# Seven products for every MLP pair, one buffer for two hidden tiles, and two low weight parts per step by ScalarE and an accumulating DMA

## The chip, the cores and the metric

The kernel runs on one core of a Trainium2 chip. The metric is the device time of one execution in microseconds (us). Three runs of the kernel before took 2107.08, 2108.14 and 2108.43 us; the median is 2108.14.

The engines are PE (TensorE, matmuls), PEld (its weight loads), DVE (VectorE), ACT (ScalarE), POOL (GpSimd, which here only issues DMAs) and SP (which issues the loads of weights). All 16 DMA engines serve the DMAs of SP and POOL.

## The reference

Two decoder layers over 256 tokens and a model width of 2048: a gated short convolution and an MLP, then shared keys and values, stick-breaking attention and a second MLP, each inside norms and a residual. The change lies in the two MLPs:

```
def sq_relu_mlp(u, w_up, w_down):
    return jnp.square(jax.nn.relu(u @ w_up)) @ w_down
```

with u of 256 x 2048, w_up of 2048 x 8192 and w_down of 8192 x 2048, in float32.

## The kernel before

**Two parts.** Each float32 factor is split into a rounded high part and a low part, the rest. A product is three matmuls: high by high, high by low, low by high. For weights, `high_parts` has ACT write the rounded copy (`whi`, L173), and `low_part` has DVE subtract it from the raw weight (`wlo`, L184).

**The stream of weights.** All weights come in chunks of 128 x 1024 (512 KB), in the order of use. SP loads them into five raw buffers (`RAW`, L157), in order. A raw buffer is free once both parts of its chunk are made. The parts lie in a ring of seven high and seven low buffers (`RING`). `chunk(i)` splits up to four chunks ahead of the one that PE uses (`AHEAD`).

**The steps of an MLP.** The 8192 hidden columns are cut into eight blocks of 8 tiles of 128 (`STEPS`). In step e, for e = 0 to 6, PE makes block e + 1 of the hidden layer (up) and multiplies block e by its rows of w_down (down), so the two alternate. A step has two halves h = 0 and 1, for the two halves of the output columns, and a half has four slots: `whole_up` makes one hidden tile from two chunks (16 matmuls of 512 columns at L1013 with high parts, 16 of 256 columns at L1020 with low parts), then `Down.pair` multiplies two hidden tiles by two chunks. A step thus takes 32 chunks, numbered from its base: in each slot two of up, then two of down. The up tile always uses PSUM bank 2 (`UP_BANK`); ACT copies its second half (`half`, L1026), DVE adds that to the first (`s`, L966), and only then may the next up tile start in that bank.

**Eight or seven products.** A pair of hidden tiles by a pair of weight chunks is a 2 x 2 by 2 x 2 block product: the token blocks by the tiles, the tiles by column halves. `Down.eight` does it in eight products. `Down.seven` does it in seven by a scheme with sums of blocks: of the weights, four differences on DVE (L210, in `split_seven`), and of the hidden tiles, four sums (`four_sums`, L271). There are 512 + 3 x 1024 weight columns to split then, in place of 2 x 1024. `SEVEN` says which pairs of which step take seven: in even steps all four, in odd steps pairs 1 to 3, while pair 0 takes eight, in both halves. Pair 0 comes first in half 0 and last in half 1 (`ORDER`). In step 7 pair 0 takes seven in the first half alone, in another order of work.

**Hidden tiles.** `Hidden.tile` makes relu and square on ACT in a buffer `s` of 256 columns (three of them), then splits. Of a seven pair, the even tile has its first 128 columns split by themselves, the odd tile is split whole, and then the four sums are made and split (128 and 384 columns). A pair with eight has a difference per tile (`dif`, L984) split.

**Results.** The products of the scheme that belong to several outputs are copied by ACT once per step (L1088) and added into the running results by nine accumulating DMAs of 256 KB, which POOL issues (`add_behind`, L1033), one at each up tile and each pair that follows: eight of them in half 1, the ninth at the start of half 0.

**Order.** PE runs in the order of the program. The other engines' instructions are ordered by a planner from their priorities and estimated times; each engine then runs its list in order.

Of the kernel before, what the change touches and what calls it, by code (L numbers as in the profile page):

```python
# [46 lines left out]
STEPS = 8  # L47
# [1 line left out]
UP_BANK = 2  # L49
DOWN_BANKS = {(0, 0): 3, (0, 1): 4, (1, 0): 5, (1, 1): UP_BANK, 1: 6, 5: 7, 6: 0, 7: 1}  # L50
LAST_BANKS = [[6, 7], [0, 1]]
SEVEN = [((0, 1, 2, 3),) * 2 if e % 2 == 0 else ((1, 2, 3),) * 2 for e in range(STEPS - 1)] + [((0,), ())]
ORDER = ((0, 1, 2, 3), (1, 2, 3, 0))

IN_N = [j * KD + i for i in range(KD) for j in range(3)]
# [40 lines left out]
def trunk(ctx, tc, x, xT, vecs, rows, ws, out):  # L96
    nc = tc.nc
# [49 lines left out]
    sevens = {}  # L147

    def load_one():
        i = count["loaded"]  # L150
# [10 lines left out]
    def pieces_of(i):  # L161
        w, c = stream[i]
        gains = w.gains(c) if w.gains else [None] * (4 if i < FIRST else 1)
        n = CW // len(gains)
        return [(slice(j * n, (j + 1) * n), gain) for j, gain in enumerate(gains)]

    def high_parts(i):
        while count["loaded"] <= i:
            load_one()
        hi = wsplit.tile([P, CW], F32R, tag="hi", name=f"whi{i}")  # L170
        lo = wsplit.tile([P, CW], F32R, tag="lo", name=f"wlo{i}")
        for j, (at, gain) in enumerate(pieces_of(i)):
            rounded = nc.scalar.activation(  # L173
                hi[:, at], raw[i][:, at], AF.Copy, scale=1.0 if gain is None else gain
            )
# [77 lines left out]
    def split_tile(xs, k, src):  # L253

        hi, lo = xs[k // 4][:, k % 4, 0, :, :], xs[k // 4][:, k % 4, 1, :, :]
        src = src.rearrange("p (b t) -> p b t", b=NB)
        nc.scalar.activation(hi, src, AF.Copy)
        nc.vector.tensor_tensor(lo, src, hi.bitcast(F32), op=ALU.subtract)
# [428 lines left out]
    W = {"in": Weights(ws["in"]), "out": Weights(ws["out"])}  # L687
# [235 lines left out]
    with tc.tile_pool(name="p_in", bufs=1, reuse_waits="tile") as tmp:  # L923
        y = convolution(tmp)
# [14 lines left out]
    def mlp(pool, i, before, after):  # L939
        u = before.x4  # L940
        part = [[None] * 4 for _ in range(NB)]
        held = {}
        scale = [None] * NB

        def two_parts(parts, src):
            hi, lo = parts
            nc.scalar.activation(hi, src, AF.Copy)
            nc.vector.tensor_tensor(lo, src, hi.bitcast(F32), op=ALU.subtract)

        class Hidden:  # L950


            def __init__(self, e):
                self.xs, self.sums = [None] * (NF // 4), {}
                first, second = SEVEN[e]
                self.pairs = [2 * m for m in first]
                self.apart = [2 * m for m in first if m not in second]
                self.eights = [2 * m for m in range(4) if m not in first] if e < STEPS - 1 else []

            def x(self, n, b):  # L960
                return [part_of(self.xs, n, b, j) for j in range(2)]

            def tile(self, n, ps, half):
                s = pool.tile([P, T], F32, tag="s", name="s", bufs=3)
                with tc.high_priority():
                    nc.vector.tensor_tensor(s[:], ps[:, :T], half[:], op=ALU.add)  # L966
                nc.scalar.activation(s[:], s[:], AF.Relu)  # L967
                nc.scalar.activation(s[:], s[:], AF.Square)
                if self.xs[n // 4] is None:
                    self.xs[n // 4] = operand("hid4")  # L970
                if n in self.pairs and n not in self.apart:
                    two_parts(self.x(n, 0), s[:, :P])
                else:
                    split_tile(self.xs, n, s[:])
                if n in self.pairs:
                    held[n] = s
                elif n - 1 in self.pairs:
                    self.sums[n - 1] = self.sums_of(n - 1, held.pop(n - 1), s)
                elif n - n % 2 in self.eights:
                    if n % 2 == 0:  # L980
                        self.sums[n] = pool.tile([P, 2, 2, P], F32R, tag="d", name="sums", bufs=1)
                    parts = [self.sums[n - n % 2][:, n % 2, j, :] for j in range(2)]
                    d = pool.tile([P, P], F32, tag="dif", name="dif", bufs=1)
                    nc.vector.tensor_tensor(d[:], s[:, :P], s[:, P:], op=ALU.subtract)  # L984
                    two_parts(parts, d[:])

            def sums_of(self, n, x, y):
# [3 lines left out]
                if n in self.apart:  # L991
                    one = pool.tile([P, 2, 2, P], F32R, tag="d", name="sums", bufs=1)
                    one = [one[:, 0, j, :] for j in range(2)]
# [112 lines left out]
        class Down:  # L1106


            def __init__(self, j, plan):
                self.j, self.plan, self.ps = j, plan, {}  # L1110
                sevens_at = [at for at in plan if at[1] in SEVEN[at[0]][at[2]]]
                whole_at = [at for at in plan if at not in sevens_at and at[0] == STEPS - 1]
# [6 lines left out]
            def products(self, key, own, at, factors):  # L1119

                begin, end = self.range[own]
                if key not in self.ps:
                    self.ps[key] = bank(DOWN_BANKS[key], "acc" if own == "sum" else "more")
                for n, ((xh, xl), (hi, lo)) in enumerate(factors):
                    first, last = at == begin and n == 0, at == end and n == len(factors) - 1
                    nc.tensor.matmul(self.ps[key][:], xh, hi, start=first, stop=False)  # L1126
                    nc.tensor.matmul(self.ps[key][:], xh, lo, start=False, stop=False)  # L1127
                    self.done = nc.tensor.matmul(self.ps[key][:], xl, hi, start=False, stop=last)  # L1128

            def pair(self, at, first, xs):  # L1130
# [23 lines left out]
            def eight(self, at, first, xs, n):  # L1154
                ws = [chunk(first + t) for t in range(2)]

                def products(key, own, x, c):
                    self.products(key, own, at, [
                        (x(t), [w[:, c * HALF : (c + 1) * HALF] for w in ws[t]]) for t in range(2)
                    ])  # L1160

                products((0, 0), "sum", lambda t: xs.x(n + t, 0), 0)
                products((1, 0), "sum", lambda t: xs.x(n + t, 1), 0)
                if at[0] == STEPS - 1:
                    products((0, 1), "sum", lambda t: xs.x(n + t, 0), 1)
                    products((1, 1), "whole", lambda t: xs.x(n + t, 1), 1)
                else:
                    products((0, 1), "sum", lambda t: [xs.sums[n][:, t, j, :] for j in range(2)], 1)
                    products(5, "fifth", lambda t: xs.x(n + t, 1), 1)
# [314 lines left out]
```

## Time and profile before

| | |
|---|---|
| median of three runs | 2108.14 us |
| profiled execution | 2106.03 us |
| its span, first to last instruction | 2104.3 us |
| its mean granted PE clock | 0.998 |

The profile gives busy times as shares of the span. A row of a view by line names a line of the kernel, an engine, the operation, what it writes and reads, a count, and times. A timeline row has the start and the length in us from the span's start; consecutive instructions overlap by some 0.08 us, so the distance of starts says what an engine pays for one. PE rows of the same line stand merged. In the timelines chunk names are numbers: step 4 of the first MLP has its base at 272. The name `wlo282u` is a low part of the pair of chunks 282 and 283: a for the first half of 282, b for 283, t and u for the differences. `more` and `mg` are the results that the accumulating DMAs read and write, `raw` the loaded weights.

### The profile page before, as it was taken

What the parts mean: (1) busy time and instruction counts of PE and PEld (TensorE: products, weight loads), DVE (VectorE), ACT (ScalarE), POOL (GpSimd) and SP (SyncE); (2) the same over time, 40 slices, a digit from 0 to 9 for tenths busy, and PEclk for the clock granted to TensorE, in tenths of its full rate; (3) what the DMA queues carried; (4) which work ended last, traced back from release to release, by engine and by line L of the source; (5) the groups of instructions that cost most, each with busy time, mean ns of one, the idle gap of its engine ahead of it and who ended that gap; (6) DMA issues with size and microseconds to landing.
All of it is one profiled execution on the core that took longest, in us unless ns stands there. A gap on an engine that the chain in (4) does not pass through costs nothing.

```text
span 2104.3 us, 29885 instructions
## 1 busy us (share of the span) xinstructions
PE 2089.1 (99%) x10608; PEld 1782.1 (85%) x10608; DVE 1837.6 (87%) x2807; ACT 1437.4 (68%) x2210; POOL 112.9 (5%) x137
## 2 busy tenths in 40 slices
PE   9999999999999999999999999999999999999998
PEld 7888888888888888888888888889888888888886
DVE  8999965999899999999766777558999999999997
ACT  8666544776776776767567888547867767677673
POOL 0000000000100101001000000000001010010010
PEclk9999999999999999999999999999999999999999
DMA  8467674577878868779575555655687687786784
GB/s 291 151 205 250 196 258 143 187 234 229 233 220 233 248 204 244 229 228 257 180 224 168 160 160 161 220 179 171 187 254 227 217 248 221 228 253 208 231 241 162
DMA packets 132342, 449.23 MB, mean 213 GB/s; under 512 B 14816, under 2 KB 15072, under 8 KB 131168
## 3 DMA queue, kind: packets, MB, share of 16 engines
q1 hardware_dynamic: 113184, 406.55, 60.1%
q0 software_dynamic: 18720, 40.38, 9.5%
q8 instruction: 83, 1.36, 0.3%
q14 instruction: 67, 0.55, 0.1%
q10 hardware_dynamic: 288, 0.39, 0.1%
HBM read 413.19 MB, written 2.10 MB: 197 GB/s over the span
## 4 chain that ended last, share of the span: by engine, by line
PE 96%; DVE 3%; issue 0%; DMA 0%; ACT 0%; SPq 0%; DVEq 0%; ACTq 0%
PE up L1013 21%; PE up L1020 12%; PE acc L326 8%; PE acc L328 8%; PE acc L327 8%; PE acc L748 5%; PE more L1127 5%; PE more L1126 5%; PE more L1128 5%; PE acc L1126 5%; PE acc L1127 4%; PE acc L1128 4%; PE lead L748 1%; PE up L1015 1%; PE tr L263 1%; DVE wlo L184 1%
## 5 line engine op out<-in xcount | busy, mean ns | idle before, releaser
L184 DVE TENSOR_TENSOR wlo<-raw,whi 128x1024 fp32r<-128x1024 f32 (+1 forms) x442 | 528.2, 1205 | 96.0 <-ACT whi L173 91.0
L173 ACT ACTIVATE whi<-raw 128x1024 fp32r<-128x1024 f32 (+1 forms) x442 | 454.5, 1044 | 172.8 <-PE acc L328 81.8
L1013 PE MATMUL up<-u,whi 128*128 128x512 f32 x1952 | 464.9, 389 | 0.0
L1013 PEld LDWEIGHTS up<-u,whi 128*128 128x128 f32 x1952 | 365.0, 188 | 74.7
L1020 PEld LDWEIGHTS up<-u,wlo 128*128 128x128 f32 x2048 | 263.6, 191 | 10.3
L1020 PE MATMUL up<-u,wlo 128*128 128x256 f32 x2048 | 268.1, 283 | 0.0
L186 DVE SCALAR_TENSOR_TENSOR wlo<-raw,gv,whi 128x512 fp32r<-128x512 f32 (+1 forms) x160 | 131.8, 854 | 41.4 <-ACT whi L173 40.7
L210 DVE TENSOR_TENSOR sums<-raw,sums 128x512 f32<-128x512 f32 x236 | 161.6, 685 | 1.3
L173 ACT ACTIVATE whi<-raw,gv 128x512 fp32r<-128x512 f32 (+1 forms) x160 | 121.7, 801 | 48.3 <-PE acc L328 41.9
L326 PE MATMUL acc<-whi,u 128*128 128x512 f32 x384 | 153.1, 399 | 0.1
L328 PE MATMUL acc<-whi,u 128*128 128x512 f32 x384 | 149.9, 390 | 0.0
L327 PE MATMUL acc<-wlo,u 128*128 128x512 f32 x384 | 149.7, 390 | 0.0
L1033 POOL DMA_DIRECT2D mg<-more x108 | 94.2, 872 | 829.9 <-ACT more L1088 425.3
L1026 ACT ACTIVATE half<-up 128x256 f32<-128x256 f32 x128 | 48.7, 382 | 99.3 <-PE up L1020 96.2
L748 PE MATMUL acc<-u,whi 128*128 128x512 f32 x416 | 98.9, 391 | 2.7 <-DVE sum L757 2.7
L748 PEld LDWEIGHTS acc<-u,whi 128*128 128x128 f32 x416 | 77.4, 188 | 20.5 <-DVE sum L757 3.7
L210 DVE TENSOR_TENSOR sums<-raw,raw 128x512 f32<-128x512 f32 x118 | 80.8, 685 | 13.8 <-DMA raw<-w_mlp 13.8
L210 DVE TENSOR_TENSOR sums<-raw 128x512 f32<-128x512 f32 x118 | 80.8, 685 | 5.7 <-DMA raw<-w_mlp 5.3
L328 PEld LDWEIGHTS acc<-whi,u 128*128 128x128 f32 x384 | 72.1, 188 | 15.5
L967 ACT ACTIVATE s<-s 128x256 f32<-128x256 f32 x128 | 52.3, 412 | 47.2 <-DVE s L966 45.9
L326 PEld LDWEIGHTS acc<-whi,u 128*128 128x128 f32 x384 | 72.2, 188 | 13.9 <-ACT tk L1316 0.6
L327 PEld LDWEIGHTS acc<-wlo,u 128*128 128x128 f32 x384 | 72.3, 188 | 13.2
(5995 smaller groups left out, 4508.4 us busy)
## 6 DMA issues: line engine op xcount, KB each, us to landing
raw<-w_mlp SPq DMA_DIRECT2D x512, 512.0 KB, 4.7
raw<-w_in SPq DMA_DIRECT2D x94, 512.0 KB, 4.4
mg<-more POOLq DMA_DIRECT2D x108, 256.0 KB, 6.5
raw<-w_out SPq DMA_DIRECT2D x32, 512.0 KB, 4.5
raw<-w_v SPq DMA_DIRECT2D x32, 512.0 KB, 4.4
raw<-w_k SPq DMA_DIRECT2D x32, 512.0 KB, 4.4
raw<-w_q SPq DMA_DIRECT2D x32, 512.0 KB, 4.3
raw<-w_wo SPq DMA_DIRECT2D x32, 512.0 KB, 3.7
```

The lines of the kernel that those rows point to most:

```text
L173: rounded = nc.scalar.activation(hi[:, at], raw[i][:, at], AF.Copy, scale=1.0 if gain is None else gain)
L184: nc.vector.tensor_tensor(lo[:, at], t[:, at], hi[:, at].bitcast(F32), op=ALU.subtract)
L210: nc.vector.tensor_tensor(t, x, y, op=ALU.subtract)
L326: nc.tensor.matmul(ps[:], xh, hi[:, a], start=i == 0 and k == 0, stop=False)
L327: nc.tensor.matmul(ps[:], xh, lo[:, a], start=False, stop=False)
L328: nc.tensor.matmul(ps[:], xl, hi[:, a], start=False, stop=i == self.n - 1 and k == self.ks - 1)
L748: nc.tensor.matmul(ps[:, :cols], w, xs[:, :cols], start=k == 0 and part == parts[0], stop=k == KD - 1 and part == parts[1], skip_group_che ...
L1013: nc.tensor.matmul(ps, weight(0, first, m), x, start=k == 0, stop=False)
L1020: nc.tensor.matmul(pss[n][:, :T], weight(1, first, m), x, start=False, stop=k == KD - 1)
L1126: nc.tensor.matmul(self.ps[key][:], xh, hi, start=first, stop=False)
L1127: nc.tensor.matmul(self.ps[key][:], xh, lo, start=False, stop=False)
L1128: self.done = nc.tensor.matmul(self.ps[key][:], xl, hi, start=False, stop=last)
```

## The change

Every pair of steps 0 to 6 takes seven products, in both halves; step 7 stays. Six pairs change (pair 0 of steps 1, 3 and 5, in two MLPs), each in two halves.

Two hidden tiles share one buffer of 2 x 256 columns (two buffers). For a seven pair the split waits for the odd tile. Then the four sums are made; the one that is a factor itself is written over the block that it replaces, and the buffer's 512 columns are split by one ACT and one DVE instruction.

Of each step 0 to 6, chunks 5 and 13 (up weights of the second and the fourth slot of half 0) get their low part in another way: ACT writes the negated rounded weight into the low buffer, and POOL issues a DMA that adds the raw chunk to it.

```diff
-SEVEN = [((0, 1, 2, 3),) * 2 if e % 2 == 0 else ((1, 2, 3),) * 2 for e in range(STEPS - 1)] + [((0,), ())]
+SEVEN = [((0, 1, 2, 3),) * 2] * (STEPS - 1) + [((0,), ())]
...
-            if not count["apart"]:
+            if i in subtracted:
+                nc.scalar.activation(lo[:, at], raw[i][:, at], AF.Copy, scale=-1.0)
+                nc.gpsimd.dma_start(lo[:, at].bitcast(F32), raw[i][:, at], accum_op=ALU.add)
+            elif not count["apart"]:
                 low_part(hi, lo, raw[i], at, gain)
...
             def tile(self, n, ps, half):
-                s = pool.tile([P, T], F32, tag="s", name="s", bufs=3)
+                if n % 2 == 0:
+                    held[n] = pool.tile([P, 2, T], F32, tag="s", name="s", bufs=2)
+                both = held[n - n % 2]
+                s = both[:, n % 2, :]
                 with tc.high_priority():
-                    nc.vector.tensor_tensor(s[:], ps[:, :T], half[:], op=ALU.add)
+                    nc.vector.tensor_tensor(s, ps[:, :T], half[:], op=ALU.add)
...
-                if n in self.pairs and n not in self.apart:
-                    two_parts(self.x(n, 0), s[:, :P])
-                else:
-                    split_tile(self.xs, n, s[:])
-                if n in self.pairs:
-                    held[n] = s
-                elif n - 1 in self.pairs:
-                    self.sums[n - 1] = self.sums_of(n - 1, held.pop(n - 1), s)
-                elif n - n % 2 in self.eights:
...
+                if n - n % 2 in self.apart or n - n % 2 not in self.pairs:
+                    split_tile(self.xs, n, s)
+                if n % 2:
+                    del held[n - 1]
+                    if n - 1 in self.pairs:
+                        self.sums[n - 1] = self.sums_of(n - 1, both)
+
+            def sums_of(self, n, both):
 
                 t = after.dump()
-                four_sums([t[:, j * P : (j + 1) * P] for j in range(4)], x[:, :P], x[:, P:], y[:, :P], y[:, P:])
...
+                s2, s3, s4 = (t[:, j * P : (j + 1) * P] for j in range(3))
+                a11, a21, a12, a22 = (both[:, j // 2, j % 2 * P : (j % 2 + 1) * P] for j in range(4))
+                apart = n in self.apart
+                s1 = t[:, 3 * P :] if apart else a21
+                for to, v, w, op in (
+                    (s3, a11, a21, ALU.subtract), (s1, a21, a22, ALU.add),
+                    (s2, s1, a11, ALU.subtract), (s4, a12, s2, ALU.subtract),
+                ):
+                    nc.vector.tensor_tensor(to, v, w, op=op)
...
                 else:
                     one = self.x(n, 1)
+                    hi, lo = (self.xs[n // 4][:, n % 4 : n % 4 + 2, j] for j in range(2))
+                    two_parts((hi, lo), both[:].rearrange("p k (b t) -> p k b t", b=NB))
...
-                two_parts(one, t[:, :P])
-                two_parts(more, t[:, P:])
+                two_parts(more, t[:, : 3 * P])
...
         for e in range(STEPS):
+            if e < STEPS - 1:
+                subtracted.update(W["mlp", i, e + 1].base + n for n in (5, 13))
```

More of the change, by code (lines that the diff above doesn't have):

```diff
@@ L147, in trunk @@
     sevens = {}
+    subtracted = set()
     def load_one():
@@ L957, in __init__ @@
                 self.apart = [2 * m for m in first if m not in second]
-                self.eights = [2 * m for m in range(4) if m not in first] if e < STEPS - 1 else []
             def x(self, n, b):
@@ L963, in tile @@
             def tile(self, n, ps, half):
-                s = pool.tile([P, T], F32, tag="s", name="s", bufs=3)
+                if n % 2 == 0:
+                    held[n] = pool.tile([P, 2, T], F32, tag="s", name="s", bufs=2)
+                both = held[n - n % 2]
+                s = both[:, n % 2, :]
                 with tc.high_priority():
-                    nc.vector.tensor_tensor(s[:], ps[:, :T], half[:], op=ALU.add)
-                nc.scalar.activation(s[:], s[:], AF.Relu)
-                nc.scalar.activation(s[:], s[:], AF.Square)
+                    nc.vector.tensor_tensor(s, ps[:, :T], half[:], op=ALU.add)
@@ L969, in tile @@
+                nc.scalar.activation(s, s, AF.Relu)
+                nc.scalar.activation(s, s, AF.Square)
                 if self.xs[n // 4] is None:
                     self.xs[n // 4] = operand("hid4")
-                if n in self.pairs and n not in self.apart:
-                    two_parts(self.x(n, 0), s[:, :P])
-                else:
-                    split_tile(self.xs, n, s[:])
-                if n in self.pairs:
-                    held[n] = s
-                elif n - 1 in self.pairs:
-                    self.sums[n - 1] = self.sums_of(n - 1, held.pop(n - 1), s)
-                elif n - n % 2 in self.eights:
[L980 to L985, printed above, removed]
@@ L987, in sums_of @@
-            def sums_of(self, n, x, y):
-                t = after.dump()
-                four_sums([t[:, j * P : (j + 1) * P] for j in range(4)], x[:, :P], x[:, P:], y[:, :P], y[:, P:])
-                if n in self.apart:
-                    one = pool.tile([P, 2, 2, P], F32R, tag="d", name="sums", bufs=1)
-                    one = [one[:, 0, j, :] for j in range(2)]
+                if n - n % 2 in self.apart or n - n % 2 not in self.pairs:
[4 more added lines that the diff above has]
+                        self.sums[n - 1] = self.sums_of(n - 1, both)
@@ new lines, in sums_of @@
+            def sums_of(self, n, both):
+                t = after.dump()
+                s2, s3, s4 = (t[:, j * P : (j + 1) * P] for j in range(3))
[7 more added lines that the diff above has]
+                    nc.vector.tensor_tensor(to, v, w, op=op)
+                if apart:
+                    one = pool.tile([P, 2, P], F32R, tag="d", name="sums", bufs=1)
+                    one = [one[:, j, :] for j in range(2)]
+                    two_parts(one, s1)
@@ L1163, in eight @@
                 products((1, 0), "sum", lambda t: xs.x(n + t, 1), 0)
[L1164 to L1169, printed above, removed]
+                products((0, 1), "sum", lambda t: xs.x(n + t, 0), 1)
+                products((1, 1), "whole", lambda t: xs.x(n + t, 1), 1)
                 spent(4 * UNIT)
         for e in range(STEPS):
+            if e < STEPS - 1:
+                subtracted.update(W["mlp", i, e + 1].base + n for n in (5, 13))
             for h in range(2):
```

## The prediction

> **What bounds the kernel now.** I read the busy times first, then the chain of work that ended last, then busy times by stretch over the MLP steps, then the timelines of one step.
>
> ```profile
> PE 2089.1 (99%) x10608; PEld 1782.1 (85%) x10608; DVE 1837.6 (87%) x2807; ACT 1437.4 (68%) x2210; POOL 112.9 (5%) x137
> ...
> PE 96%; DVE 3%; issue 0%; DMA 0%; ACT 0%; SPq 0%; DVEq 0%; ACTq 0%
> ...
> 406.08:988.47 582.39, 582.39 (x2987) 499.65 (x2987) 554.41 (x813) 421.13 (x649) 52.36 (x60) 1.00 0.77 228
> 1470.57:2052.98 582.41, 582.41 (x2988) 499.64 (x2987) 554.24 (x813) 420.72 (x649) 52.37 (x60) 1.00 0.77 228
> ```
>
> The last two rows are the seven pipelined steps of the first and of the second MLP; the columns are length, then busy time of PE, PEld, DVE, ACT and POOL, the granted clock, the DMA share and GB/s. PE is busy for the whole length at clock 1.00: it never waits there. So matmuls taken away come out of the end one for one, as long as nobody makes PE wait instead. DVE is close behind, 554.3 of 582.4 us (95%), and is the engine to watch. Single steps of the first MLP show what a pair costs:
>
> ```profile
> 739.27:821.89 82.62, 82.62 (x426) 70.91 (x425) 80.15 (x114) 61.31 (x93) 7.85 (x9) 1.00 0.78 222
> 821.89:905.86 83.97, 83.97 (x431) 72.02 (x431) 77.77 (x119) 56.83 (x90) 7.85 (x9) 1.00 0.79 237
> ```
>
> The first is step 4, in which all eight pair visits take seven products; the second is step 5, where two of the eight (pair 0, once in each half) take eight.
>
> **PE, the part that pays.** An eight-product visit has 24 matmuls (L1126 to L1128), a seven-product visit 21. A step with two of the former is 83.97 - 82.62 = 1.35 us longer, so three matmuls are 0.675 us, 0.225 each. Steps 1, 3 and 5 change in both MLPs: 6 x 1.35 = 8.1 us. Nothing else on PE changes; the banks and the number of evictions stay.
>
> **DVE, the part that pays for it.** A timeline of DVE in step 4 (start, length):
>
> ```profile
> 751.33 1.22 DVE L184 TENSOR_TENSOR wlo<-raw,whi 128x1024 fp32r<-128x1024 f32 x1
> 752.46 0.69 DVE L210 TENSOR_TENSOR sums<-raw 128x512 f32<-128x512 f32 x1
> 753.07 0.69 DVE L210 TENSOR_TENSOR sums<-raw,raw 128x512 f32<-128x512 f32 x1
> 753.67 1.41 DVE L210 TENSOR_TENSOR sums<-raw,sums 128x512 f32<-128x512 f32 x2
> 755.00 1.22 DVE L184 TENSOR_TENSOR wlo<-raw,whi 128x1024 fp32r<-128x1024 f32 x1
> 756.13 0.42 DVE L966 TENSOR_TENSOR s<-up,half 128x256 f32<-128x256 f32 x1
> ...
> 759.48 0.28 DVE L984 TENSOR_TENSOR dif<-s 128x128 f32<-128x128 f32 x1
> 759.70 1.23 DVE L184 TENSOR_TENSOR wlo282u<-sums,whi282u 128x1024 fp32r<-128x1024 f32 x1
> 760.84 0.42 DVE L258 TENSOR_TENSOR hid<-s,hid 128x256 fp32r<-128x256 f32 x1
> 761.18 0.29 DVE L948 TENSOR_TENSOR sums<-dif,sums 128x128 fp32r<-128x128 f32 x1
> ```
>
> From start to start, 1024 columns take 1.13 us, 512 take 0.61, 256 take 0.34, 128 take 0.21. That spacing is what DVE really pays.
> - Weights. An eight-product visit splits two chunks: 2 x 1.13 = 2.27. A seven-product visit makes four differences and splits 512 and three times 1024 columns: 5 x 0.61 + 3 x 1.13 = 6.43. Extra 4.16, twelve times: 49.9 us.
> - Hidden tiles. Per seven pair a split of 512 columns (0.61) stands for 128 + 256 + 128 (0.76): 0.15 saved, 50 times, 7.5 us. A former eight pair cost 2 x 0.34 + 4 x 0.21 = 1.52 and now costs 4 x 0.21 + 0.61 + 0.47 for 384 columns (between its neighbours) = 1.92: 0.4 more, six times, 2.4 us.
> - The offload. Chunks 5 and 13 of the 32 of each step lose their subtraction: 2 x 7 x 2 = 28 times 1.13 = 31.7 us.
>
> Together +13.1 us on 1108.7, in a stretch that shrinks by 8.1 to 1156.7: DVE goes from 95.2% to 97.0%. It stays under PE. Steps of the all-seven kind, which DVE already keeps up with at 80.15 of 82.62, become lighter by 2.27; the light ones become like them. ACT gains 12 x (0.64 + 1.06) for the extra splits and 28 x 1.06 for the negated copies, about 50 us on 842: 77%, off the path.
>
> ```profile
> L173 ACT ACTIVATE whi<-raw x20: 1043/1062/1068, 740.2 to 820.6; 128x1024 fp32r<-128x1024 f32 x20
> L218 ACT ACTIVATE whi282a<-raw x1: 636/636/636, 753.3 to 753.3; 128x512 fp32r<-128x512 f32 x1
> ```
>
> **The new chain.** A low part of an offloaded chunk was one DVE subtraction. Now ACT writes the negated rounded weight into the low buffer, then POOL issues a DMA of 512 KB that adds the raw weight to it. Three things wait for its landing: PE's low matmuls, and the raw buffer of the chunk, which was freed by DVE and now by the DMA; SP loads in order into five such buffers, so the loads behind it wait too, and the differences on DVE after them. Take chunk 277 in step 4 (the fifth after 272).
>
> ```profile
> 740.17 2.02 ACT L173 ACTIVATE whi<-raw 128x1024 fp32r<-128x1024 f32 x2
> ...
> 742.74 2.08 PE L1020 MATMUL up<-u,wlo 128*128 128x256 f32 x16
> ...
> 745.11 1.22 DVE L184 TENSOR_TENSOR wlo<-raw,whi 128x1024 fp32r<-128x1024 f32 x1
> ...
> 746.36 0.33 SPq L157 DMA_DIRECT2D raw<-w_mlp  x1
> ...
> 753.07 2.08 PE L1020 MATMUL up<-u,wlo 128*128 128x256 f32 x16
> ...
> 759.77 3.79 PE L1013 MATMUL up<-u,whi 128*128 128x512 f32 x16
> ```
>
> The low buffer comes from a ring of seven, six of them taken in each slot (one up tile and one pair, 10.33 us), so 277 takes over that of 272, which PE reads in the first half of the row at 742.74, until 743.9. ACT can then write 743.9 to 745.0 (1.06), and POOL issues at 745.1. PE wants the result in the second half of the row at 753.07: 754.0. **The budget from issue to landing is 8.9 us.** What lands how fast (KB, median us to landing; first the half of the step with chunks 5 and 13, then the other half; last the spread of all 122):
>
> ```profile
> raw<-w_mlp SPq DMA_DIRECT2D x16, 512.0 KB, 4.1
> mg<-more POOLq DMA_DIRECT2D x1, 256.0 KB, 3.5
> ...
> raw<-w_mlp SPq DMA_DIRECT2D x17, 512.0 KB, 5.8
> mg<-more POOLq DMA_DIRECT2D x7, 256.0 KB, 6.4
> ...
> DMA to landing us min/median/max: 3.3/6.5/8.7
> ...
> 739.27:780.58 41.31, 41.31 (x214) 35.45 (x213) 40.37 (x56) 29.80 (x45) 0.87 (x1) 1.00 0.66 205
> 780.58:821.89 41.31, 41.31 (x214) 35.45 (x213) 39.78 (x59) 31.50 (x49) 6.98 (x8) 1.00 0.90 239
> ```
>
> The second half has seven accumulations more, and 0.24 x 41.31 = 9.9 us more of DMA time: 1.4 us for 256 KB. No accumulation of 512 KB is in the trace. Its bounds: 3.3 (the extra bytes free) and 8.7 + 1.4 = 10.1 (the slowest, plus the bytes). I take 3.5 + 1.4, about 5: it runs in the half with one other accumulation and a DMA share of 0.66 (two of these add 2 x 2.8 / 41.3 = 0.14). It lands at 750.1, 3.9 us before PE wants it. No stall there.
>
> By the Trainium skill, page "DMA: Bandwidth & Descriptors", section "Anatomy of one DMA — SWDGE (gpsimd) path", such a DMA takes 2.0 us plus bytes at 436 GB/s, which I estimate as 3.2 us here, with the same sum; the quiet 256 KB accumulation already took 3.5 where that rule gives 2.6, so the trace decides.
>
> The raw buffer is the tighter end. The next load into it, chunk 282, leaves SP at 746.36 now (when the subtraction of 745.11 ends) and at about 750.2 then; at 4.1 us it lands at 754.3, and 283 some 1.3 us behind. DVE starts the differences of 282 at 752.46 today, without 277's subtraction at 751.3: it will idle up to 3 us, finish the four at about 757.4, do 281's low part until 758.5 and the addition L966 by 759.2. That addition frees the one up bank, and PE starts the next up tile at 759.77. **About 0.5 us is left.** So I cost the offload at nothing on PE; what hides it is that half microsecond and DVE's lead over PE (wlo282u is done at 760.9, PE needs it at about 769). If that cover is gone, each microsecond of lateness costs up to 28 us. DVE regains its lag at 10.33 - 10 us in each of the next slots and by 1.13 at each offload.
>
> **The sum.** 2106.03 is the profiled execution's time (span 2104.3 and 1.7 around it); 2106.0 - 8.1 = 2097.9. The median shown is 2.1 above it: 2108.14 - 8.1 = **2100.0**.
>
> **Rivals.**
> 1. *The up bank comes late.* As above: 282 and 283 land late, L210 holds up L966 in DVE's order, PE waits for bank 2. For it: the 0.5 us. Against: ACT and DVE are ordered by a planner, which can put the addition before the differences, as it has priority. Equal to no change at 8.1 / 28 = 0.29 us a time, slower beyond; at 1 us 2100 + 28 = 2128. At the upper bound (landing 755.2, differences done at 762.4, addition at 764.2) 4.4 us, 2223, but that bound is a row of the busy half.
> 2. *DVE becomes the bound.* A step needs 82.62 x 0.97 = 80.1 us of DVE, and two idle spells of 3 us would make it 86.1. Against: once DVE lags by such a spell, the next one finds it late already and costs nothing; so at most 1 to 2 us a step remain, 14 steps, 2114 to 2128.
> 3. *Issue on POOL is starved.* DVE is never free for long, and a descriptor writer that it blocks would issue late. Here the price is whatever passes the 0.5 us: with 2.5 us more per DMA, 2.0 x 28 = 56, so 2156. Against it stands that 122 issues took 862 to 907 ns beside the same DVE:
>
> ```profile
> L1033 POOL DMA_DIRECT2D mg<-more x108: 862/872/895, 454.8 to 2053.3; - x108
> L1033 POOL DMA_DIRECT2D more<-more x14: 872/872/907, 452.1 to 2017.9; - x14
> ```
>
> The Trainium skill, page "SBUF — State Buffer", section "SBUF: two separate sides", has the rule: a DVE instruction that holds the shared port pair keeps GpSimd from writing descriptors. It gives 620 ns against 3100, whence the 2.5 us; the rows do not show it, with DVE on two-tensor subtractions.
>
> 4. *The gain is not there*: PE waits about as much as it saves, 2104 to 2112.
>
> **Chances.** Forecast 0.64, between 2098.5 and 2102; rival 1 0.16; rival 2 0.09; rival 3 0.03; rival 4 0.08. No change that can be told is within 0.2%, 4.2 us. Faster: the forecast and a few mild cases of rival 1, 0.66. Same: 0.08. Slower: 0.26. The range takes the forecast, rival 4 and the cases of rivals 1 and 2 up to 1 us a time: 2098 to 2128; beyond lie perhaps 0.13 above and 0.04 below.
>
> **What would show it.** Right: all fourteen steps last 82.6 us with PE busy throughout; DVE at 80 to 81 us in each; L184 subtractions of raw weights fewer by 28; new 512 KB accumulations on POOL that land in 4.5 to 6 us; DVE waits before L210 for raw weights that grow from today's
>
> ```profile
> DVE sums L210 <- DMA raw<-w_mlp: 19.1, 25, 1.8
> ```
>
> (us in all, times, longest). Wrong: gaps on PE before L1013 for L966 (rival 1), before L1126 to L1128 for a low part by DVE (rival 2), before L1020 for a DMA (the budget of 8.9), or POOL issues far over 0.9 us (rival 3).

## The result and the profile after

The changed kernel takes 2132.19 us (median of four runs, 2126.45 to 2134.12); the kernel before took 2108.28 in the runs beside it (2107.08 to 2112.55). The ratio is 1.0108, with a 95% interval from 1.0095 to 1.0122: slower by some 24 us, where 8 us less were forecast. The profiled execution took 2134.12 us, span 2132.3.

Busy times and the shares of the chain of work that ended last, from the page of the changed kernel:

```profile
PE 2095.9 (98%) x10572; PEld 1773.1 (83%) x10572; DVE 1846.3 (87%) x2751; ACT 1444.9 (68%) x2150; POOL 137.0 (6%) x165
...
PE 55%; DVE 27%; DMA 12%; issue 4%; ACT 2%; DVEq 0%; SPq 0%; ACTq 0%
```

Its windows over the seven pipelined steps of the first and of the second MLP (columns as in the prediction):

```profile
409.43:1003.60 594.17, 584.55 (x2970) 494.34 (x2969) 557.51 (x790) 422.98 (x619) 64.43 (x74) 1.00 0.82 235
1485.72:2080.80 595.08, 584.97 (x2970) 494.27 (x2969) 557.01 (x789) 421.78 (x619) 64.45 (x74) 1.00 0.82 234
```

PE lost its 36 matmuls, and the clock is still 1.00, but the chain, 96% PE before, now runs over DVE and DMA for 39%. The forecast had 14 steps of 82.6 us, 1156.7 in all; they take 594.17 + 595.08 = 1189.25, so 32.6 us are lost here, the whole distance from the forecast of 2100. The steps of PE are no longer busy from end to end: in the two windows PE stands idle for 19.7 us, and its busy time is 1169.5 us, 12.8 more than the forecast's 1156.7.

The view of waits for the whole run (us, times, longest; PEld is the load of weights ahead of the matmuls) says for whom PE waits:

```profile
DVE sums L214 <- DMA raw<-w_mlp: 68.9, 53, 2.9
...
PEld up L1020 <- DVE s L972: 38.2, 47, 2.0
...
PE up L1020 <- DVE s L972: 18.7, 23, 1.6
```

L972 (L966 before) is the addition that frees the up bank, L1020 (L1013 before) the first matmul of the next up tile, L214 (L210 before) the differences of the weights. DVE waits for raw weights 3.6 times as long as before (68.9 against 19.1), and PE then waits for DVE's addition, a wait that the kernel before did not have.

One place shows how the two are tied. This is the chain that ended last within step 4 of the first MLP, from 757 to 772 us (start, length, what; PE's up tile had started at 759.42, so the next one is due 10.33 later, at 769.75):

```profile
758.55 0.34 DVE s L972
758.89 0.61 DVE wlo278a L188
759.50 0.02 SPq L158
...
759.55 4.94 DMA raw<-w_mlp
...
764.58 0.06 DVE sums L214
764.64 0.55 issue
765.19 1.22 DVE wlo L188
766.41 1.22 DVE sums L214 x2
...
768.26 1.22 DVE wlo L188
769.48 0.60 DVE wlo282a L188
770.08 0.35 DVE s L972
```

Read it from the top: DVE splits chunk 278; only then does a raw buffer come free; the load of chunk 282 leaves at 759.55 and lands 4.94 us later; DVE, whose list has the differences of 282 next, waits, starts them at 764.58 and goes on through its list; the addition stands last in it. Its operands had been there since ACT's copy ended at 765.54, 4.5 us earlier (timeline of ACT):

```profile
765.16 0.38 ACT L1033 ACTIVATE half<-up 128x256 f32<-128x256 f32 x1
```

PE starts its next up tile at 770.47, 0.7 us late, of which 0.56 are idle time (timeline of PE):

```profile
770.47 3.92 PE L1020 MATMUL up<-u,whi 128*128 128x512 f32 x16 [0.56 <-DVE s L972]
```

Its 16 matmuls take 3.92 us where the prediction's row of L1013 has 3.79, so a late tile costs more than PE's idle time alone.

Behind the late load stands the held buffer. From the timelines of POOL and SP, the issue of chunk 277's accumulation, 2.4 us ahead of the slot, and a load that leaves 5.8 us later:

```profile
757.01 0.87 POOL L181 DMA_DIRECT2D wlo<-raw  x1 [6.59 <-ACT half L1033]
...
762.78 0.33 SPq L158 DMA_DIRECT2D raw<-w_mlp  x1
```

The view of DMAs, with the median from issue to landing, first for all 28 of the changed kernel, then for this one:

```profile
wlo<-raw POOLq DMA_DIRECT2D x28, 512.0 KB, 5.1
...
wlo<-raw POOLq DMA_DIRECT2D x1, 512.0 KB, 5.8
```

757.01 + 5.8 is 762.8, when that load (of chunk 284) leaves. So one of the five raw buffers is away from ACT's negated copy to the landing, and the load of 282, which before left 3.1 us ahead of its slot (746.36 against 749.44), now leaves 0.1 us after its start, when DVE has split 278.

### The profile page after: what moved, and what is told of

It is laid out like the page before. It is cut to its first block, busy times and chain, and to the rows that moved or that the text cites. A ratio compares the mean times of both kernels' runs of the same rounds, so it can differ in the third digit from the quotient of the medians.

```text
span 2132.3 us, 29710 instructions
## 1 busy us (share of the span) xinstructions
PE 2095.9 (98%) x10572; PEld 1773.1 (83%) x10572; DVE 1846.3 (87%) x2751; ACT 1444.9 (68%) x2150; POOL 137.0 (6%) x165
## 4 chain that ended last, share of the span: by engine, by line
PE 55%; DVE 27%; DMA 12%; issue 4%; ACT 2%; DVEq 0%; SPq 0%; ACTq 0%
DMA raw<-w_mlp 11%; PE up L1020 9%; DVE wlo L188 8%; PE acc L330 7%; PE acc L332 7%; PE acc L331 7%; DVE sums L214 7%; PE up L1027 5%; PE acc L752 3%; PE more L1134 2%; PE more L1133 2%; PE lead L752 2%; PE more L1135 2%; PE acc L1133 1%; PE acc L1134 1%
## 5 line engine op out<-in xcount | busy, mean ns | idle before, releaser
L188 DVE TENSOR_TENSOR wlo<-raw,whi 128x1024 fp32r<-128x1024 f32 (+1 forms) x390 | 467.9, 1208 | 83.6 <-ACT whi L174 83.0
L174 ACT ACTIVATE whi<-raw 128x1024 fp32r<-128x1024 f32 (+1 forms) x418 | 421.9, 1040 | 126.7 <-PE acc L332 82.3
L1020 PE MATMUL up<-u,whi 128*128 128x512 f32 x1952 | 471.6, 393 | 19.7 <-DVE s L972 18.7
L1020 PEld LDWEIGHTS up<-u,whi 128*128 128x128 f32 x1952 | 361.3, 188 | 111.2 <-DVE s L972 38.2
L214 DVE TENSOR_TENSOR sums<-raw,sums 128x512 f32<-128x512 f32 x260 | 180.1, 693 | 2.1
L214 DVE TENSOR_TENSOR sums<-raw 128x512 f32<-128x512 f32 x130 | 90.3, 695 | 39.3 <-DMA raw<-w_mlp 39.0
L214 DVE TENSOR_TENSOR sums<-raw,raw 128x512 f32<-128x512 f32 x130 | 90.2, 693 | 30.4 <-DMA raw<-w_mlp 29.9
L181 POOL DMA_DIRECT2D wlo<-raw x28 | 24.5, 874 | 659.7 <-ACT half L1033 622.5
```

Of the source, the lines that this page charges most:

```text
L174: rounded = nc.scalar.activation(hi[:, at], raw[i][:, at], AF.Copy, scale=1.0 if gain is None else gain)
L188: nc.vector.tensor_tensor(lo[:, at], t[:, at], hi[:, at].bitcast(F32), op=ALU.subtract)
L214: nc.vector.tensor_tensor(t, x, y, op=ALU.subtract)
L1020: nc.tensor.matmul(ps, weight(0, first, m), x, start=k == 0, stop=False)
```

## The experiments

Each edit is against the changed kernel, unless it says against the kernel before. Medians of the kernel before in the four groups of runs (the first four experiments, the next four, three, one) were 2107.65, 2108.13, 2107.62 and 2109.04 us. Brackets hold the 95% interval of a ratio to it.

**Take the accumulating DMA away.** The low part stays the negated high part.

```diff
-                nc.gpsimd.dma_start(lo[:, at].bitcast(F32), raw[i][:, at], accum_op=ALU.add)
```

> The changed kernel without the 28 accumulating DMAs: ACT still writes the negated copy, DVE still skips the subtraction, nothing adds the raw weight (the low parts of chunks 5 and 13 are left as the negated high parts). Theory H (the DMA holds the raw buffer, the loads behind it come late, DVE waits for them, the add that frees the up bank comes late): the 33 us of DVE waits on raw weights in the first MLP fall to under 10, time 2098 to 2104. Theory L (DVE has too much work with seven products everywhere, whoever makes the low parts): DVE work is the same, so 2125 to 2135. Theory B (the split that waits for the odd tile delays ACT and DVE): 2125 to 2135 as well.

Measured: 2099.0 us (2098.08 to 2100.04), ratio 0.9956 [0.9941, 0.9970]. DVE waits 10.5 us for raw weights. The DMA alone, with ACT's copies still there, is what costs 33 us. In the trace the list of DVE is that of the changed kernel, all 2751 instructions in the same order (buffer numbers left out). So with this list and loads in time nothing is lost: in the place shown above, the addition comes 6.6 us into its slot (755.37, the slot starts at 748.77).

**Take the raw weights from HBM**, so that the DMA doesn't hold the raw buffer, at the price of 512 KB more to read.

```diff
-                nc.gpsimd.dma_start(lo[:, at].bitcast(F32), raw[i][:, at], accum_op=ALU.add)
+                w, c = stream[i]
+                nc.gpsimd.dma_start(lo[:, at], w.ap[c, :, at].bitcast(F32R), accum_op=ALU.add)
```

> The accumulating DMA reads the weights from HBM in place of the raw buffer, so the raw buffer is free as soon as ACT has read it twice; the low part still lands by the same kind of DMA. 28 x 512 KB = 14.7 MB more are read from HBM. H: waits on raw weights nearly gone, 2098 to 2108. A rival within H, that the low part itself lands too late for PE or that the DMA traffic slows the loads: stays at 2120 to 2135. L and B: 2125 to 2135.

Measured: 2120.12 us (2115.28 to 2122.40), 1.0053 [1.0037, 1.0069]. In the views of waits and of DMAs:

```profile
DVE sums L215 <- DMA raw<-w_mlp: 52.6, 54, 2.2
PEld up L1028 <- DMA wlo<-w_mlp: 14.2, 15, 2.4
PE up L1028 <- DMA wlo<-w_mlp: 10.9, 12, 2.2
```

```profile
wlo<-w_mlp POOLq DMA_DIRECT2D x28, 512.0 KB, 8.0
```

A third of the loss went, with DVE's list again that of the changed kernel, and another wait came: landing in 8.0 us, the DMA uses up nearly all of the 8.9 us that the prediction allowed it, and PE waits for the low part itself (L1028 there). The wait at the addition has nearly gone (1.8 us), but DVE still waits for raw weights for 52.6 us: holding the buffer is not the only way in which the DMA makes loads late.

**All of the change but the offload**, and then **the offload alone**, in the kernel before.

```diff
-                subtracted.update(W["mlp", i, e + 1].base + n for n in (5, 13))
+                subtracted.update(W["mlp", i, e + 1].base + n for n in ())
```

> The changed kernel with no chunk offloaded: DVE makes all low parts again, 28 x 1.13 = 31.7 us more DVE work, 577 of 578 us per MLP. H: the raw waits go, but DVE is full: 2100 to 2115. L: slower than the changed kernel, 2140 or more. B: as the changed kernel or slower.

Measured: 2099.89 us (2098.64 to 2100.28), 0.9958 [0.9941, 0.9974]. The forecast of 2100.0 is the time of this kernel. The offload thus costs 2132.19 - 2099.89 = 32.3 us beside it.

> The kernel before with only the offload of chunks 5 and 13 added (no more seven products, separate buffers). DVE work falls by 31.7 us. H: DVE waits on raw weights rise from 8 to 25 us or more per MLP, and with the lighter odd steps part of it reaches PE: 2110 to 2125. L: DVE is lighter, no slower than before: 2105 to 2109. B: 2105 to 2109.

Measured: 2110.21 us (2107.48 to 2114.94, ten runs), 1.0012 [1.0003, 1.0021]. The same 28 DMAs cost 2.6 us there. DVE waits for raw weights for 55.5 us, nearly as long as in the changed kernel, and yet PE waits for the addition for 0.6 us. So the late loads as such don't make PE wait; whether they do depends on what else DVE has to do, and where.

**Read the high part in place of the raw weight**, with the same bytes inside SBUF, but no raw buffer held; and **let PE not wait for the low part** (it reads the high part of the offloaded chunks).

```diff
-                nc.gpsimd.dma_start(lo[:, at].bitcast(F32), raw[i][:, at], accum_op=ALU.add)
+                nc.gpsimd.dma_start(lo[:, at].bitcast(F32), hi[:, at].bitcast(F32), accum_op=ALU.add)
```

> The accumulating DMA reads the chunk's rounded high part in SBUF in place of its raw buffer (so the low parts of chunks 5 and 13 become zero). Same DMA, same bytes from SBUF to SBUF, same landing for PE to wait for; but the raw buffer is free once ACT has read it twice. Theory H (the held raw buffer makes the loads late): DVE waits on raw weights fall from 69 us to 20 to 30 in all, 2099 to 2106. Theory T (the traffic of the accumulation slows the loads): 2115 to 2132. Theory P (PE's low matmuls wait for the landing): gaps on PE before L1027, 2115 to 2132.

Measured: 2109.72 us (2102.61 to 2121.22, ten runs), 1.0009 [0.9993, 1.0025], between the theories. Its view of DMAs:

```profile
wlo<-whi POOLq DMA_DIRECT2D x28, 512.0 KB, 7.8
```

DVE's list is once more that of the changed kernel. With the raw buffer free, the loads leave earlier and run beside the DMA, which lands in 7.8 us instead of 5.1; DVE still waits for raw weights for 45.2 us, and PE for low parts for 4.8. So 22 of the 32 us go with the held buffer; that the rest is traffic is argued from these landings.

```diff
-            return chunk(first + m // CH, part == 1)[part][:, m % CH * P : (m % CH + 1) * P]
+            c = first + m // CH
+            return chunk(c, part == 1)[0 if c in subtracted else part][:, m % CH * P : (m % CH + 1) * P]
```

> The changed kernel, but PE's low matmuls of chunks 5 and 13 read the high part instead of the low part, so nothing on PE waits for the landing (the product with the low part is replaced). The DMA still holds raw and low buffer. H: unchanged, 2122 to 2135, waits on raw weights 60 to 75 us. T: unchanged too. P: 2099 to 2106.

Measured: 2110.51 us (2104.96 to 2114.93, ten runs), 1.0007 [0.9995, 1.0018]. This agreed with neither side: DVE does the same work, the DMAs land in the same 5.0 us, PE never waited for a low part in the changed kernel, and still 22 us are gone. What else the edit changes is what the planner sees, and so the order of DVE's list: 180 of its 2751 instructions stand elsewhere. It was the first hint at that order; the run by itself doesn't show it.

**Half of the offload**, chunk 13 alone.

```diff
-                subtracted.update(W["mlp", i, e + 1].base + n for n in (5, 13))
+                subtracted.update(W["mlp", i, e + 1].base + n for n in (13,))
```

> Only chunk 13 of each step is offloaded, 14 instead of 28. DVE paces the MLP steps as busy time plus forced waits: per MLP 562.6 busy and 5 idle with no offload, 547 and 37 with two a step. Half way: 555 + 21 = 576 against 568 that PE needs, so 8 us an MLP, 2116. If the lag has time to be regained over six slots: 2099 to 2105. A theory that one fixed cost a DMA falls on PE: 14 x 1.15 = 16, 2116 as well, but then with PE gaps in every step beside chunk 13 alone.

Measured: 2116.44 us (2114.17 to 2119.44), 1.0039 [1.0024, 1.0054]: 16.5 us above the kernel without any, half of 32.3. So an offload costs about 1.2 us on average with one a step as with two.

**Seven products alone**: the kernel before with the one line of `SEVEN` changed, no shared buffer and no offload.

> The kernel before with seven products for every pair alone: no offload, separate buffers for the hidden tiles. DVE has 50 x 0.15 + 0.1 more to do than in the run without offload, 3.8 us per MLP: 566.4 busy of 568. If 5 us of idle time stay as they were, DVE paces: 571.6 per MLP, 2107 in all. If the idle time can shrink: 2100. If the shared buffer itself costs time by its later splits: below 2099.

Measured: 2098.57 us (2097.43 to 2099.25), 0.9953 [0.9938, 0.9968]; the 1.3 us to the kernel without offload are too little to price the shared buffer, as the two intervals overlap. Busy times of the whole run, and the window over the first MLP's seven steps:

```profile
PE 2082.1 (99%) x10572; PEld 1776.5 (85%) x10572; DVE 1877.8 (90%) x2891; ACT 1454.3 (69%) x2234; POOL 112.6 (5%) x137
```

```profile
407.25:985.57 578.32, 578.32 (x2971) 496.22 (x2970) 575.00 (x855) 430.88 (x660) 52.24 (x60) 1.00 0.79 229
```

DVE is busy for 575.0 of 578.3 us (99.4%), and PE, at 578.32 of 578.32, does not wait for it. So the relief that the offload and the shared buffer give to DVE meets no need.

**The order of DVE's list.** The four differences of a pair are put behind the latest addition that frees the up bank (from the first such addition on).

```diff
-        for t, x, y in ((t1, b12, b11), (t3, b22, b12), (t2, b22, t1), (t4, b21, t2)):
-            nc.vector.tensor_tensor(t, x, y, op=ALU.subtract)
+        def differences():
+            for t, x, y in ((t1, b12, b11), (t3, b22, b12), (t2, b22, t1), (t4, b21, t2)):
+                nc.vector.tensor_tensor(t, x, y, op=ALU.subtract)
+        if last_add[0] is None:
+            differences()
+        else:
+            with tc.issue_after(last_add[0].ins):
+                differences()
...
-                    nc.vector.tensor_tensor(s, ps[:, :T], half[:], op=ALU.add)
+                    last_add[0] = nc.vector.tensor_tensor(s, ps[:, :T], half[:], op=ALU.add)
```

> The changed kernel with an order edge on DVE: the four differences of a pair of weight chunks stand behind the addition that frees the up bank, not ahead of it. Theory O (only the order costs: the add waits behind differences that wait for raw weights): PE no longer waits for the add, 2100 to 2108. Theory D (each offload makes DVE idle for more than the subtraction that it saves, and DVE paces the steps wherever it idles): 2120 to 2140, with the PE waits moved to the products of the pairs.

> The same order edge without any offload, the control for the run before. D: as without the edge, 2098 to 2104, unless the edge itself makes DVE idle for the up tile's copy; its own price is then the difference to 2099.9 and is taken off the run before. O: 2098 to 2104.

Measured: 2112.15 us with the offload (2107.08 to 2114.94, eight runs), 1.0021 [1.0011, 1.0032]; 2101.42 without it (2098.98 to 2103.35, six runs), 0.9969 [0.9958, 0.9981]. The edge alone takes 20 of the 32 us away, which leaves e9 between the two theories. The windows over the second to seventh step of each MLP say more, first with the offload (e9), then without (e10):

```profile
498.02:994.66 496.64, 496.19 (x2545) 425.44 (x2544) 474.88 (x667) 370.54 (x522) 55.81 (x64) 1.00 0.84 243
1565.68:2061.33 495.65, 495.65 (x2545) 425.33 (x2544) 475.32 (x668) 371.87 (x524) 55.90 (x64) 1.00 0.84 243
```

```profile
492.99:988.66 495.67, 495.67 (x2545) 425.33 (x2544) 489.39 (x683) 363.73 (x512) 45.36 (x52) 1.00 0.80 232
1553.48:2049.15 495.67, 495.67 (x2545) 425.33 (x2544) 489.83 (x683) 364.08 (x512) 45.39 (x52) 1.00 0.79 232
```

With the same accumulations, PE is busy for 495.65 of 495.65 us in the second MLP (496.19 of 496.64 in the first), and DVE has 14.5 us less to do in each. The offload costs 1.0 us in the first MLP's six steps and nothing in the second's. What is left of its cost lies in the first step of each MLP, where e9 has one long stall each. The timeline of the first MLP's (POOL's issue, PE's wait):

```profile
441.26 0.89 POOL L182 DMA_DIRECT2D wlo<-raw  x1 [22.81 <-ACT s L980]
...
449.29 1.71 PE L1034 MATMUL up<-u,wlo 128*128 128x256 f32 x8 [4.19 <-DMA wlo<-raw]
```

Weights are split with little lead in the first step: the DMA left at 441.26, PE was in the rows that want its result when it stopped, and stood for 4.19 us.

**The other half of the step**, chunks 21 and 29 in place of 5 and 13, where eight of the nine accumulations of results run, without the edge.

```diff
-                subtracted.update(W["mlp", i, e + 1].base + n for n in (5, 13))
+                subtracted.update(W["mlp", i, e + 1].base + n for n in (21, 29))
```

> The changed kernel with chunks 21 and 29 offloaded in place of 5 and 13, that is in half 1, where eight accumulations of 256 KB run besides and the DMA engines are 0.9 busy. D with the loads as its cause: loads behind the DMA later still, more forced idle time, 2135 to 2160. If the place doesn't matter: 2125 to 2135.

Measured: 2162.76 us (2156.82 to 2164.40), 1.0254 [1.0237, 1.0271], 2.8 us above the upper end of what D expected. The waits of PE at the addition, and now some for the low part too:

```profile
PEld up L1020 <- DVE s L972: 44.0, 23, 4.0
PE up L1020 <- DVE s L972: 34.8, 17, 3.6
...
PE up L1027 <- DMA wlo<-raw: 7.8, 4, 2.8
```

Without the edge this half is the worse place, though the accumulations themselves land in 5.7 us. DVE waits for raw weights for 95.6 us there; that the busier DMA engines are the reason is not shown. Part of the loss is PE's clock, which has a mean of 0.991 there and of 0.998 in the changed kernel. With the edge this place wasn't tried.

**The edge, and no offload in the first step.** This decides whether e9's last 10.7 us are a price of every offload (D) or of the first steps alone (O). (The 485.3 us that the expectation gives to six steps end one slot of 10.33 short of them; the comparison in it holds for the whole six, as above.)

```diff
-            if e < STEPS - 1:
+            if 0 < e < STEPS - 1:
                 subtracted.update(W["mlp", i, e + 1].base + n for n in (5, 13))
```

> The changed kernel with the same edge as in e9_add_first (on DVE the four differences of a pair come after the addition that frees the up bank), and with the offload in every pipelined step of an MLP but the first one: 24 accumulating DMAs in place of 28. In the trace of e9_add_first the second to the seventh step of each MLP run at PE's own pace (485.3 and 486.3 us for six steps that last 485.3 without any offload), with DVE busy for 464.8 us of them; the first steps are about 6 and 7 us longer, and there PE waits up to 4.2 us for the low part of chunk 13, whose DMA left only 2.7 us ahead of the row that reads it. Theory O, the order alone made the offload dear in the steady steps, and what was left in e9 lies in the first steps: 2100 to 2103, as in e10_add_first_clean (2101.4), and no PE wait for wlo. Theory D, each offload costs idle time of DVE and of PE wherever it stands: 10.7 us x 24/28 = 9.2 above 2101.4, so 2108 to 2113. Either way it does not come under e10, as DVE, which it relieves, is not what PE waits for: under 2099 would say that DVE's relief is worth something.

Measured: 2100.51 us (2097.89 to 2101.12), 0.9957 [0.9944, 0.9971]. That is O's value: 24 accumulating DMAs, and a time like that of e10, which has none. All seven steps of the first MLP, in which PE never waits, and DVE's timeline in the place that answers to the chain shown above (its up tile started at 748.93):

```profile
408.12:986.44 578.32, 578.32 (x2970) 496.29 (x2969) 558.78 (x793) 434.63 (x619) 62.67 (x72) 1.00 0.84 241
```

```profile
753.40 2.36 DVE L189 TENSOR_TENSOR wlo<-raw,whi 128x1024 fp32r<-128x1024 f32 x2
755.67 0.69 DVE L189 TENSOR_TENSOR wlo282a<-raw,whi282a 128x512 fp32r<-128x512 f32 x1
756.27 0.42 DVE L979 TENSOR_TENSOR s<-up,half 128x256 f32<-128x256 f32 x1
756.61 0.68 DVE L216 TENSOR_TENSOR sums<-raw 128x512 f32<-128x512 f32 x1
757.21 0.69 DVE L216 TENSOR_TENSOR sums<-raw,raw 128x512 f32<-128x512 f32 x1
757.81 0.69 DVE L216 TENSOR_TENSOR sums<-raw,sums 128x512 f32<-128x512 f32 x1
```

The addition (L979 there) starts 7.3 us after its up tile, and the differences behind it at 7.7, with no wait in front of them. In the changed kernel the differences stood ahead of the addition, 5.2 us into the slot, and waited; the addition came at 10.6. The loads land no earlier here. That of 282 left at 748.74, 0.2 us ahead of the slot, took 5.7 us, and so landed 5.5 us into it (5.1 in the changed kernel). That of 283 left at

```profile
752.37 0.33 SPq L159 DMA_DIRECT2D raw<-w_mlp  x1
```

as the accumulation issued at 745.73 landed, 6.6 us later; that is 3.4 us into the slot, where the changed kernel has it leave 1.2 us in (760.65). DVE just asks for the weights later. And no version with the offload is faster than the kernels without it and without the edge: the best is the single line of e8, 2098.57.

Left open: how much of e6 was its edit and how much the order that the planner then chose. In e1, e2 and e5 the order on DVE and ACT is that of the changed kernel, so there it is the landings that differ. A sixth raw buffer wasn't tried.

## Why the prediction was wrong

**PE's 8.1 us were right.** Without the offload the kernel takes 2099.9, with seven products alone 2098.6: 7.8 and 9.6 us below the kernel before in the same runs.

**DVE's sum was right in its conclusion and too high in its terms.** It gave 44.8 us more DVE work without the offload (49.9 - 7.5 + 2.4) and 31.7 back from it. Busy time in the whole run grew by 1872.1 - 1837.6 = 34.5 us in e3, and the changed kernel has 1872.1 - 1846.3 = 25.8 less. "It stays under PE" holds even at 99.4%. ACT was to gain about 50 us and gained 7.5 (1444.9 against 1437.4); no term of the forecast hangs on it.

**The budget of 8.9 us was right for the step it was read from.** The accumulation was put at about 5 us and lands in 5.1; in the changed kernel no wait of PE for a low part shows. (With the edge the first steps have less: the 4.19 us stall of e9.) By the fit that the prediction took from the Trainium skill, page "DMA: Bandwidth & Descriptors", section "Anatomy of one DMA — SWDGE (gpsimd) path", the estimate was 3.2; the measurement is 5.1 here and 6.7 in e12.

**The step that failed is the end of the raw-buffer paragraph: "About 0.5 us is left. So I cost the offload at nothing on PE; what hides it is that half microsecond and DVE's lead over PE".** Three things in it were wrong.
- The list between load and addition. Its times for the load were close: 282 was to land at 754.3, 4.9 us into its slot, and landed at 764.49, 5.1 into it, though not by the way described (it waited for DVE's split of 278; the held buffer went to a load two places on). But behind it I counted four differences, one low part and the addition, which was to be done 9.8 us into the slot. In the trace stand two low parts and wlo282a ahead of the addition, which starts at 10.6. My working took the list of the kernel before and struck out the low part at 751.33 as chunk 277's. It is not: 277's is the one at 745.11, whose end lets the load at 746.36 go, as the same paragraph says. The one at 751.33 stays; it stood ahead of the differences before, and in the changed kernel it stands behind the first of them, and wlo282a ahead of the addition. At the spacing of the prediction that is 1.13 + 0.61 us more behind the load, against 0.5 left.
- Who regains the lag. "DVE regains its lag at 10.33 - 10 us in each of the next slots and by 1.13 at each offload" takes DVE's inputs as fixed. But a load leaves when DVE has split an earlier chunk, as that of 282 did at 759.55, so it moves with DVE, and the time that DVE waits for it is lost anew: 53 waits in the run, against 25 before.
- The price. The prediction did say that each microsecond of lateness would cost up to 28 us. It is 32.6 / 28 = 1.16 us an offload.

**Rival 1 was the right one, and its counter-argument decided the matter.** Its sign, gaps on PE before the up tile for the addition, is what the waits show. "At 1 us 2100 + 28 = 2128" was 0.16 us an offload short of the result. Against it I had written that the planner "can put the addition before the differences, as it has priority". It did not, and where an edge made it do so, with the offload from the second step on, the time was 2100.5. The forecast describes a kernel with another order on DVE and no offload in the first steps: with that order and all 28 offloads e9 takes 2112.15. The prediction read its slack in step 4 and took it for all fourteen. I could have checked the order in the rows that I quoted myself: in step 4 of the kernel before, the differences start at 752.46 and the addition follows at 756.13.

**Rival 2** (DVE becomes the bound) had the idle spells of DVE right, 68.9 us of waits for raw weights. Its sign, PE waiting for a low part at the products (L1133 to L1135 now), does not show in the changed kernel, its price of 2114 to 2128 lies below the result, and DVE's work is not the bound: it keeps PE fed at 99.4% in e8. **Rival 3** (POOL's issue starved) is refuted; in the groups of the changed kernel its issues take 874 ns on average, like the accumulations before:

```profile
L181 POOL DMA_DIRECT2D wlo<-raw x28 | 24.5, 874 | 659.7 <-ACT half L1033 622.5
```

**Rival 4** (the gain is not there) is refuted by e3 and e8.

## What to carry to other kernels

When an in-order engine waits for a late input, list what stands behind the waiting instruction before pricing the wait at the slack that is left: here an addition that had been ready for 4.5 us stood behind subtractions that were not, and with the other order the same DMAs cost at most 1.0 us in an MLP outside its first step. Relieving an engine pays only where another waits for it; DVE at 99% busy was no bound, so neither the offload nor the shared buffer could gain. Count a buffer as held for as long as its slowest reader has it: a DMA in place of a subtraction held one of five for more than 5 us in place of 1.2.

## What the runs showed of the hardware that was not expected

- An engine can be busy for 99.4% of a stretch (DVE, 575.00 of 578.32 us in e8) with PE never waiting for it.
- The same 512 KB of accumulation took a median of 5.0 us to land in e6, 5.1 in the changed kernel, 6.7 in e12, and 7.8 and 8.0 in e5 and e2, whose source wasn't the raw buffer. How busy the DMA engines are doesn't settle it alone: in the busy half of e11 it was 5.7.
- A stall of PE can cost more than its length. Windows of e9 over its stall in the first MLP, the first of them the stall itself (the third number from the end is the granted clock):

```profile
444.00:449.20 5.20, 1.10 (x9) 0.89 (x7) 4.76 (x5) 2.13 (x3) 0.00 (x0) 1.00 1.02 258
449.75:453.17 3.42, 3.42 (x13) 2.94 (x12) 1.72 (x4) 1.65 (x3) 0.00 (x0) 0.50 0.80 274
453.17:458.00 4.83, 4.83 (x22) 3.97 (x22) 4.01 (x8) 4.63 (x10) 0.00 (x0) 1.00 0.66 242
```

After 4.2 us without work the granted clock was 0.50 for 3.42 us, then 1.00 again, and from up tile to up tile the slot took 16.36 us in place of 10.33. The length of a wait alone doesn't decide it: a wait of 2.22 us that ended at 848.26 in e2 was followed by such a stretch, while one of 2.90 us that ended at 736.08 in e11 was not:

```profile
848.30:851.60 3.30, 3.30 (x12) 3.01 (x13) 2.40 (x5) 0.38 (x1) 0.00 (x0) 0.50 0.59 201
730.00:740.00 10.00, 7.11 (x33) 5.56 (x32) 8.12 (x11) 5.46 (x9) 1.74 (x2) 1.00 0.95 277
```

The waits of up to 1.6 us in the changed kernel left its mean over the steps at 1.00. The Trainium skill, page "TensorE: Matmul & The Clock Gate", section "Part 1: The HAM clock gate (the "warmup" mystery)", has the clock halved after an idle window of about 3.4 us; the trace agrees on the half clock, and e2's 2.22 us show that a wait shorter than that can be enough.
